# Cached keys of the second decode unit requested one unit earlier, forgetting-attention weights turned back into their row tiles

## The chip, the cores and the metric

The kernel runs on one core of a Trainium2 chip. A core has five engines that run side by side, each with its own queue of instructions, worked off in order: TensorE (PE: matmuls, and the loads of their weights, PEld), VectorE (DVE), ScalarE (ACT), GpSimd (POOL) and SyncE (SP), which here issues all DMA transfers. Engines wait for one another by semaphores. The metric is the device time of one execution, in microseconds (us); smaller is better.

## The reference

One step of a hybrid trunk of one layer, on 1024 new prompt rows and on 8 streams of 16 sample rows each, all in float32. Three token mixers run on one normalised input: a stick-breaking attention, a state-space scan (SSD) and a forgetting attention (fox). What matters here are the two attentions of the sample rows over 1024 cached rows per stream:

```python
def sb_attend(q, k, v, q_pos, k_pos):
    z = jnp.einsum('bqhd,bkhd->bhqk', q, k).astype(jnp.float32) * (HEAD_DIM ** -0.5)
    valid = k_pos[None, :] < q_pos[:, None]
    log_keep = jnp.where(valid, jax.nn.log_sigmoid(-z), 0.0)
    after = lax.cumsum(log_keep, axis=3, reverse=True) - log_keep
    w = jnp.where(valid, jnp.exp(jax.nn.log_sigmoid(z) + after), 0.0)
    return jnp.einsum('bhqk,bkhd->bqhd', w, v.astype(jnp.float32)).astype(q.dtype)

def fox_attend(q, k, v, fq, fk, q_pos, k_pos):
    s = jnp.einsum('bqhd,bkhd->bhqk', q, k).astype(jnp.float32) * (HEAD_DIM ** -0.5)
    s = s + (jnp.transpose(fq, (0, 2, 1))[..., :, None] - jnp.transpose(fk, (0, 2, 1))[..., None, :])
    valid = k_pos[None, :] <= q_pos[:, None]
    p = jax.nn.softmax(jnp.where(valid, s, -jnp.inf), axis=-1)
    return jnp.einsum('bhqk,bkhd->bqhd', p, v.astype(jnp.float32)).astype(q.dtype)
...
    logf = jax.nn.log_sigmoid((fg + p['fox_b_f']).astype(jnp.float32))
...
        sb_k = jnp.concatenate([past['sb_k'].astype(sk.dtype), sk], axis=1)
        sb_o = sb_attend(sq, sb_k, sb_v, qpos, kpos)
        fcum = jnp.cumsum(jnp.concatenate([past['fox_logf'].astype(jnp.float32), logf], axis=1), axis=1)
        fox_o = fox_attend(fq, fox_k, fox_v, fcum[:, past_len:], fcum, qpos, kpos)
```

Behind the mixers come an output projection, a cross-attention and a feed-forward part, which the change doesn't touch.

## The kernel before

In the mixed stage (which ends at about 705 us) attention units are interleaved with a filler. `mixed` makes a list of units for each attention, m = 0 stick-breaking and m = 1 fox: 16 prompt units (two blocks of 128 rows of one head each) and four decode units, whose places `AT0` and `AT1` give. A decode unit takes two streams and has two parts. `rows` computes its scores against two halves of 512 cached keys (`emit_past`) and the new ones (`emit_new`, L942 and L943), by L905 into a PSUM tile `pss`, and turns them into weights in a row tile `w` of 128 x 1152, out of a pool of seven (`ws`). `av`, a unit or two later, transposes these weights on PE (L965) into PSUM, ACT copies them out (L966), and L974 multiplies them with the cached values (`vr`, L983).

For m = 0 the cached keys are read in an arrangement of 128-byte pieces, four requests of 128 KB to a tile `kf` (L871), and DVE turns them in place (L910). A half needs two such tiles, `wh` and `wl` of one ring of three slots each, which also holds the high and low parts of the projection weights (`w_unit`: load to `wr`, L327; cast on ACT, L295; subtraction on POOL, L133) and the cached values. `fetch` asks for a unit's first half ahead of time: `mixed` hangs it on the unit in front of the decode unit. The second half is asked for in `emit_past`.

The filler `fill_s` gives the input projections in turn (fox queries and keys, `proj_v` with values and forget gates, z, the conv inputs), then the SSD scan `ssd_gen`. Behind `proj_v`, whose consumer adds the gates to `lf` (L505), `fox_sums` turns them into cumulated log gates: a logarithm in short steps on DVE (L418 to L426, with seven L424), L673, and matmuls L697 and L698 on PE; L699 copies and L705 transposes them. The matmuls of the projections are L341 to L343, three for each product of high and low parts.

Large tiles `act` (128 x 3072, six of them) hold the normalised input in its parts, the loads of the SSD blocks (L1078 to L1082), and, for each fox unit, a tile `hold` with the spread queries `qt`, the transposed weights `wt` and `wn`. For m = 0 those lie in smaller tiles (`st`, `sg2`). The tile `sc` of `ssd_gen` is a further `act` tile.

The order of each engine's queue is set by a scheduler from the program's order, priorities and modelled costs, which also gives the slots of a pool to the tiles; so a small edit can move many instructions. A load waits until the slot of its tile is free. No more than eight DMAs are on the way: each one waits for the one eight before it.

Of the kernel before, what the change touches and what calls it, by code (L numbers as in the profile page):

```python
# [8 lines left out]
F32 = mybir.dt.float32  # L9
# [8 lines left out]
P = 128  # L18
# [5 lines left out]
PAST = 1024  # L24
T = SEQ + DEC_B * DEC_S
# [38 lines left out]
def tile_hybrid_step(ctx: ExitStack, tc: tile.TileContext, a: dict):  # L64
# [22 lines left out]
    def act_t(dt=F32R, home=None):  # L87
        return (home or actp).tile([P, 3072], dt, tag="act", name="act")
# [4 lines left out]
    def st_t(dt=F32R):  # L93
        return stp.tile([P, 1024], dt, tag="st", name="st")
# [47 lines left out]
    rows = xc_t()  # L142
# [63 lines left out]
    fnew = mcst.tile([P, P], F32, name="fnew")  # L206
# [417 lines left out]
    def sg2_t(dt=F32):  # L624
        return ptp.tile([P, 256], dt, tag="so", name="so", bufs=4)
# [42 lines left out]
    fqs = mcst.tile([P, 4], F32, name="fqs")  # L668
# [189 lines left out]

    def decode_units(m):
        ck = (a["cache_sb_k"], a["cache_fox_k"])[m][0].rearrange("b k h d -> b k (h d)")
        cv = (a["cache_sb_v"], a["cache_fox_v"])[m][0].rearrange("b k h d -> b k (h d)")
# [24 lines left out]
        def rows(p):  # L888
            if not new:
                load_new()  # L890
            qsm = new[0]

            hold = act_t(F32) if m else None
            qt = (hold if m else st_t(F32))[:, 0:P]
            POOL.memset(qt, 0.0)
            q0 = qsm[:, 0:2, 0, 32 * p:32 * p + 32].rearrange("p n (b t) -> p n b t", b=2)
            qp = qt.rearrange("p (b n e t) -> p n e b t", b=2, n=2, e=2)
            for par in range(2):
                r = slice(par * 64, par * 64 + 64)
                for nb in range(2):  # L900
                    POOL.tensor_copy(qp[r, nb, par], q0[r, nb])

            def quads(ps, moving):

                together([lambda g=g: PE.matmul(ps[32 * g:32 * g + 32, :], qt[:, 32 * g:32 * g + 32],  # L905
                                                moving(g // 2, g % 2), start=True, stop=True) for g in (3, 0, 1, 2)])

            def turn_k(hf, b2):
                kf = fetched.pop((p, b2)) if (p, b2) in fetched and not hf else fetch_k(p, hf, b2)
                DVE.transpose(kf, kf)  # L910
                return kf.rearrange("c (t n i) -> c n t i", t=16, n=2)

            def load_k(hf, b2):
                rvs = []
                for q in range(2):
                    rvs.append(raw_t()[:, :512].rearrange("p (k c) -> p k c", c=256))
                    k0 = hf * 512 + q * 256

                    SP.dma_start(out=rvs[q], in_=ck[2 * p + b2, k0:k0 + 256, :].rearrange("(p k) c -> p k c", k=2))
                kf = ring.tile([P, 1088], F32, tag=("wh", "wl")[b2], name="kf")  # L920
                for q in range(2):
                    tp = pT()
                    for nb in range(2):
                        for k in range(2):
                            PE.transpose(tp[:, (2 * nb + k) * P:(2 * nb + k + 1) * P], rvs[q][:, k, nb * P:(nb + 1) * P],
                                         ident)
                    ACT.copy(kf[:, :1024].rearrange("c (n q p k) -> c n q p k", n=2, q=2, k=2)[:, :, q],
                             tp.rearrange("c (n k p) -> c n p k", n=2, k=2))
                return kf

            def emit_past(hf):
                def emit(ps):
                    if m == 0:
                        kf = [turn_k(hf, b2) for b2 in range(2)]
                        quads(ps.rearrange("p (t i) -> p t i", t=16), lambda b2, nb: kf[b2][:, nb])
                        return "turned"
                    kf = [load_k(hf, b2) for b2 in range(2)]
                    quads(ps, lambda b2, nb: kf[b2][:, nb * 512:(nb + 1) * 512])
                return emit

            def emit_new(ps):
                PE.matmul(ps, identr, dmask[:, 96 - 32 * p:224 - 32 * p], start=True, stop=False)  # L942
                together([lambda g=g: PE.matmul(ps[32 * g:32 * g + 32, :], qt[:, 32 * g:32 * g + 32], qsm[:, 2 + g % 2, 0, :],  # L943
                                                start=False, stop=True) for g in range(4)])

            pieces = [(0, 512, emit_past(0)), (512, 512, emit_past(1)), (1024, P, emit_new)]
            if m == 0:
                return sb_rows(T, pieces), hold
            fkb = xc_t()
            SP.dma_start(out=fkb[:, :PAST],  # L950
                         in_=fs4[8 * p:8 * p + 8].rearrange("r i k -> (r i) k").unsqueeze(1).to_broadcast([32, 4, PAST]))
            return fox_rows(T, pieces, [(0, PAST, fkb[:, :PAST]), (PAST, P, fnew)], fqs[:, p:p + 1], frs[:, p:p + 1]), hold

        def av(p, w, hold):
            vsm = new[1]

            wt = hold[:, P:P + 1024] if m else st_t(F32)
            wn = hold[:, P + 1024:2 * P + 1024] if m else sg2_t()[:, :P]
            for k0 in (0, 4, 8):
                nk = min(4, 9 - k0)  # L960
                tp = pT()
                for k in range(nk):
                    wk = w[:, 8 * P:9 * P] if k0 == 8 else \
                        w[:, k0 * P:(k0 + 4) * P].rearrange("q (p k) -> q p k", k=4)[:, :, k]
                    PE.transpose(tp[:, k * P:(k + 1) * P], wk, ident)  # L965
                ACT.copy(wn if k0 == 8 else wt[:, k0 * P:(k0 + 4) * P], tp[:, :nk * P])  # L966

            po = pO()

            def quads(w, moving, start, stop):  # L970
                def one(g):
                    v = moving(g // 2, g % 2)
                    out = po[32 * g:32 * g + 32, :P]
                    return PE.matmul(out if len(v.shape) == 2 else out.rearrange("p (h d) -> p h d", h=2),  # L974
                                     w[:, 32 * g:32 * g + 32], v, start=start, stop=stop)
                return [lambda g=g: one(g) for g in (3, 0, 1, 2)]

            work = quads(wn, lambda b2, nb: vsm[:, 2 * nb:2 * nb + 2, 0, :], True, False)
            for hf in range(2):
                raws = []  # L980
                for b2 in range(2):
                    raw = ring.tile([P, 1088], F32, tag=("wh", "wl")[b2], name="vr")
                    SP.dma_start(out=raw[:, :1024].rearrange("p (k c) -> p k c", c=256),  # L983
                                 in_=cv[2 * p + b2, hf * 512:(hf + 1) * 512, :]
                                 .rearrange("(p k) c -> p k c", k=4))
                    raws.append(raw)
                for k in range(4):
                    work += quads(wt[:, (4 * hf + k) * P:(4 * hf + k + 1) * P],
                                  lambda b2, nb, raws=raws, k=k: raws[b2][:, k * 256 + nb * P:k * 256 + (nb + 1) * P],
                                  False, hf == 1 and k == 3)  # L990
            together(work)
            ob = sg2_t()[:, :P]
            DVE.scalar_tensor_tensor(ob.rearrange("p (h d) -> p h d", h=2), po[:, :P].rearrange("p (h d) -> p h d", h=2),
                                     frs[:, p:p + 1] if m else 1.0, maskh.unsqueeze(2).to_broadcast([P, 2, 64]),
                                     ALU.mult, ALU.mult)
            of = pT()
            PE.matmul(of[:, :64], ob, fold2.rearrange("p n t -> p (n t)"), start=True, stop=True)
            on = sg2_t()[:, :64]
            DVE.tensor_copy(on, of[:, :64])
            SP.dma_start(out=mix_sc[2 * m:2 * m + 2, :, SEQ + 32 * p:SEQ + 32 * p + 32].rearrange("n p t -> p n t"),  # L1000
                         in_=on.rearrange("p (n t) -> p n t", n=2))

        return [([lambda p=p: rows(p)], lambda w, p=p: av(p, *w[0])) for p in range(4)], fetch


    final = []

    def ssd_gen():
        sc = act_t(F32)
        hT, gB = sc[:, 0:512], sc[:, 512:1024]  # L1010
        triu, btri, ones, bones = (sc[:, 1024 + 128 * i:1152 + 128 * i] for i in range(4))
        bmask = sc[:, 1536:1544]
# [301 lines left out]
    def mixed(m, at, fc, nxt):  # L1314
# [10 lines left out]
        units, fetch = decode_units(m)  # L1325
        for i, u in reversed(list(enumerate(units))):
            if m == 0:
                rows, av = out[at[i] - 1]
                out[at[i] - 1] = ([lambda f=rows[0], i=i: (fetch(i), f())[1]] + rows[1:], av)
            out.insert(at[i], u)  # L1330
        return out, heads[0][1]

# [837 lines left out]
```

## Time and profile before

| | |
|---|---|
| time before, three runs | 1861.90, 1858.74, 1856.07 us; median 1858.74 |
| the profiled execution | 1859.39 us, its span 1857.7 us |
| busy share of the span | PE 96%, PEld 86%, DVE 49%, ACT 42%, POOL 33% |
| DMA | 289.54 MB, 156 GB/s over the span |

The profile is of one execution. Its rows name an instruction by its line, its engine, its operation and its tiles (out<-in, without the buffers' numbers). In square brackets stands how long the engine was idle ahead of it, and what ended that. A releaser is inferred: of several semaphores it is the one that came last by the profile, and it can be the wrong one where the engine named was just passing. `SPq` is the queue of SP, in which the issues of DMAs stand. The granted clock of PE is 1.00 at full speed and about 0.5 when throttled.

### The profile page before, as it was taken

Reading aid. Unit: us, or ns where it says so; the run is one execution under the profiler, and the core shown is the slowest. Engines: PE = TensorE matmul, PEld = TensorE weight load, DVE = VectorE, ACT = ScalarE, POOL = GpSimd, SP = SyncE. Lnnn points to the kernel's source line nnn. Section 1 sums busy time; section 2 is a strip of 40 time slices with the busy share of each in tenths; the row PEclk is TensorE's granted clock in tenths of the full one; section 3 lists DMA queues with packets and bytes.
Section 4 is the critical chain, followed back from the end, with each engine's and each line's share of the span. In section 5 each row is a group of like instructions: output and inputs, shape, how many; then the busy total and the mean of one; then the engine's idle time right before and its main releaser. Section 6 shows DMA issues by size and latency. Waiting matters only on the chain.

```text
span 1857.7 us, 31848 instructions
## 1 busy us (share of the span) xinstructions
PE 1791.4 (96%) x11880; PEld 1602.9 (86%) x11880; DVE 915.9 (49%) x1808; ACT 786.5 (42%) x1665; POOL 622.0 (33%) x921
## 2 busy tenths in 40 slices
PE   7999978999998989999999989999999999999998
PEld 5899867888966767899988889999999999888886
DVE  3412434576656863455553695333333334455554
ACT  6532524445455862333342564333333333344443
POOL 7623523446115673121021107444444542000000
PEclk9999998999999999999999989999999999999999
DMA  9467765566678883257873234322222233657572
GB/s 333 160 187 185 197 140 133 149 123 194 182 236 257 284 290 103 110 138 166 191 235 105 80 93 111 90 72 72 72 72 72 72 77 88 218 187 250 177 247 86
DMA packets 367499, 289.54 MB, mean 156 GB/s; under 512 B 179052, under 2 KB 323412, under 8 KB 367344
## 3 DMA queue, kind: packets, MB, share of 16 engines
q1 hardware_dynamic: 367344, 287.50, 53.3%
q8 instruction: 94, 1.54, 0.3%
q14 instruction: 61, 0.50, 0.1%
HBM read 221.58 MB, written 66.38 MB: 155 GB/s over the span
## 4 chain that ended last, share of the span: by engine, by line
PE 79%; DVE 6%; DMA 6%; POOL 3%; ACT 2%; issue 2%; SPq 1%; DVEq 0%; POOLq 0%; ACTq 0%
PE psd L1963 11%; PE psd L341 10%; PE psd L342 9%; PE psd L343 9%; PE pst L1963 8%; PE pss L1963 4%; PE pss L341 3%; PE pss L343 3%; PE pss L342 3%; PE pso L1963 2%; PE pst L342 2%; PE pst L341 2%; PE pst L343 2%; DMA act<-acsc 1%; POOL wl L133 1%
## 5 line engine op out<-in xcount | busy, mean ns | idle before, releaser
L341 PE MATMUL psd<-act,wh 128*128 128x384 f32 x528 | 182.2, 345 | 0.0
L343 PE MATMUL psd<-act,wl 128*128 128x384 f32 x528 | 179.7, 341 | 0.0
L342 PE MATMUL psd<-act,wh 128*128 128x384 f32 x528 | 179.2, 340 | 0.0
L133 POOL TENSOR_TENSOR wl<-wr,wh 128x256 fp32r<-128x256 f32 (+2 forms) x152 | 111.6, 768 | 165.1 <-ACT wh L295 135.4
L1963 PE MATMUL pst<-bT,tr 128*128 128x256 f32 (+1 forms) x1068 | 154.6, 292 | 0.0
L1963 PEld LDWEIGHTS pst<-bT,tr 128*128 128x128 f32 x1068 | 144.6, 188 | 0.1
L343 PE MATMUL psd<-wh,act 128*128 128x512 f32 (+3 forms) x424 | 135.2, 320 | 0.0
L341 PE MATMUL psd<-wh,act 128*128 128x256 f32 (+3 forms) x414 | 132.6, 324 | 1.5 <-ACT act L1442 1.3
L342 PE MATMUL psd<-wl,act 128*128 128x256 f32 (+3 forms) x414 | 132.8, 322 | 1.2 <-POOL wl L133 1.1
L1963 PE MATMUL psd<-bT,tr 128*128 128x320 f32 (+1 forms) x912 | 132.7, 295 | 0.7 <-POOL tr L133 0.7
L1963 PEld LDWEIGHTS psd<-bT,tr 128*128 128x128 f32 x912 | 124.8, 188 | 0.9 <-POOL tr L133 0.9
L133 POOL TENSOR_TENSOR ws<-ws 128x256 f32<-128x256 f32 (+2 forms) x100 | 76.2, 788 | 133.0 <-DVE ws L538 114.5
L133 POOL TENSOR_TENSOR tr<-u,tr 128x256 fp32r<-128x256 f32 x110 | 82.9, 781 | 101.1 <-ACT tr L1799 83.3
L256 POOL TENSOR_SCALAR sm<-sm 128x1 f32<-128x1 f32 (+2 forms) x27 | 9.1, 337 | 295.4 <-ACT y L2074 207.2
L1938 DVE TENSOR_TENSOR tr<-tr,pst 128x256 f32<-128x256 f32 (+1 forms) x86 | 38.6, 449 | 138.9 <-ACT tr L1935 105.8
L341 PEld LDWEIGHTS psd<-act,wh 128*128 128x128 f32 x528 | 99.5, 188 | 4.6 <-issue 3.8
L343 PEld LDWEIGHTS psd<-act,wl 128*128 128x128 f32 x528 | 99.2, 188 | 2.2 <-issue 1.9
L342 PEld LDWEIGHTS psd<-act,wh 128*128 128x128 f32 x528 | 99.4, 188 | 1.7 <-issue 1.3
L133 POOL TENSOR_TENSOR tr<-raw,tr 128x256 fp32r<-128x256 f32 x94 | 69.2, 763 | 83.6 <-ACT tr L1799 75.4
L1799 ACT CAST tr<-u 128x512 fp32r<-128x512 f32 x130 | 76.6, 620 | 28.5 <-PE pst L1963 5.9
L341 PEld LDWEIGHTS psd<-wh,act 128*128 128x128 f32 x414 | 78.9, 191 | 9.5 <-issue 1.9
L342 PEld LDWEIGHTS psd<-wl,act 128*128 128x128 f32 x414 | 78.6, 190 | 9.2 <-POOL wl L133 3.0
(646 smaller groups left out, 4621.0 us busy)
## 6 DMA issues: line engine op xcount, KB each, us to landing
u<-w_down SPq DMA_DIRECT2D x40, 512.0 KB
raw<-w_down SPq DMA_DIRECT2D x26, 512.0 KB
st<-qksc SPq DMA_DIRECT2D x48, 256.0 KB
wr<-w_in SPq DMA_DIRECT2D x44, 256.0 KB
tr<-hidsc SPq DMA_DIRECT2D x55, 192.0 KB
hidsc<-tr SPq DMA_DIRECT2D x34, 288.0 KB
qksc<-sg SPq DMA_DIRECT2D x48, 192.0 KB
kf<-cache_sb_k SPq DMA_DIRECT2D x64, 128.0 KB
```

What stands on the lines that cost most here:

```text
L133: POOL.tensor_tensor(out=out[:, a0:a1], in0=in0[:, a0:a1], in1=in1[:, a0:a1], op=op)
L256: POOL.tensor_scalar(v, ss, inv, EPS, ALU.mult, ALU.add)
L341: PE.matmul(out, ah, bh, start=start, stop=False)
L342: PE.matmul(out, ah, bl, start=False, stop=False)
L343: PE.matmul(out, al, bh, start=False, stop=stop)
L1799: ACT.copy(hi, src)
L1938: DVE.tensor_tensor(out=at(out, g), in0=at(x, g), in1=ps[g][:, :GW[g]], op=op)
L1963: PE.matmul(dst[g][:, :GW[g]], x[:, ka], y[:, k, :], start=start and k == 0 and m == 0, stop=stop and k == 3 and m == 2, skip_group_check= ...
```

## The change

Three edits. The fetch of the first half of keys for stick-breaking decode unit 1 (and this unit only) hangs on the unit two in front of it, not one. `av` copies the transposed weights back into the columns of the unit's own row tile `w`, from which they were transposed. And there is no `hold` tile: the fox queries `qt` lie in 128 columns, one of two places in turn, of a single `act` tile which `ssd_gen` uses as `sc`.

```diff
+    kept = []
+
+    def keep_t():
+        if not kept:
+            kept.append(act_t(F32))
+        return kept[0]
...
-            hold = act_t(F32) if m else None
-            qt = (hold if m else st_t(F32))[:, 0:P]
+            qt = keep_t()[:, 2456 + P * (p % 2):2456 + P * (p % 2) + P] if m else st_t(F32)[:, 0:P]
...
-        def av(p, w, hold):
+        def av(p, w):
             vsm = new[1]
-
-            wt = hold[:, P:P + 1024] if m else st_t(F32)
-            wn = hold[:, P + 1024:2 * P + 1024] if m else sg2_t()[:, :P]
+            wt, wn = w[:, 0:8 * P], w[:, 8 * P:9 * P]
...
     def ssd_gen():
-        sc = act_t(F32)
+        sc = keep_t()
...
             if m == 0:
-                rows, av = out[at[i] - 1]
-                out[at[i] - 1] = ([lambda f=rows[0], i=i: (fetch(i), f())[1]] + rows[1:], av)
+                k = at[i] - (2 if i == 1 else 1)
+                rows, av = out[k]
+                out[k] = ([lambda f=rows[0], i=i: (fetch(i), f())[1]] + rows[1:], av)
```

The number of instructions stays the same on every engine. By the trace of before, the orders differ between about 205 and 350 us and between 470 and 705 us. Lines of the changed kernel are 4 to 7 higher: L871 is L878, L910 is L916, L1000 is L1004, L1078 is L1082, L919 is L925.

On SP, behind the loads of z's first weights (220 us in the trace of before), where the keys of unit 1 were not yet in sight:

```order
L327 DMA wr<-w_in 128x2x256
L327 DMA wr<-w_in 128x2x8
L520 DMA st<-qksc 64x1024
L521 DMA st<-qksc 64x1024
L327 DMA wr<-w_in 128x2x256
L327 DMA wr<-w_in 128x2x8
L1000 DMA mixsc<-so 128x2x32
```

and in the changed kernel:

```order
L327 DMA wr<-w_in 128x2x256
L327 DMA wr<-w_in 128x2x8
L878 DMA kf<-cache_sb_k 32x32x32 x4
L1004 DMA mixsc<-so 128x2x32
L878 DMA kf<-cache_sb_k 32x32x32 x4
L327 DMA wr<-w_in 128x2x256
L327 DMA wr<-w_in 128x2x8
```

The eight requests of the first half now stand here, four on either side of the store of unit 0's result. Before, they stood behind the stores of proj_v, at 256 us.

On DVE, the logarithm of the forget gates, first as before (260 to 269 us):

```order
L422 TENSOR_SCALAR sg<-sg 128x36
L910 STREAM_TRANSPOSE kf<-kf 128x1024
L424 SCALAR_TENSOR_TENSOR sg<-sg 128x36 x7
L425 SCALAR_TENSOR_TENSOR sg<-sg 128x36
L910 STREAM_TRANSPOSE kf<-kf 128x1024
L426 TENSOR_SCALAR sg<-sg 128x36
L711 SCALAR_TENSOR_TENSOR sg<-sg 128x64 x4
L673 SCALAR_TENSOR_TENSOR lf<-lf,sg 128x36
```

and in the changed kernel, from the fourth of the seven L424 on:

```order
L424 SCALAR_TENSOR_TENSOR sg<-sg 128x36
L916 STREAM_TRANSPOSE kf<-kf 128x1024
L716 TENSOR_TENSOR so<-so,smask 128x32
L424 SCALAR_TENSOR_TENSOR sg<-sg 128x36 x3
L425 SCALAR_TENSOR_TENSOR sg<-sg 128x36
L426 TENSOR_SCALAR sg<-sg 128x36
L673 SCALAR_TENSOR_TENSOR lf<-lf,sg 128x36
L693 COPY so<-lf 128x4
L916 STREAM_TRANSPOSE kf<-kf 128x1024
```

The two transposes that stood in this chain were of the first half of keys; the ones that stand there now are of the second half. The two of the first half moved up, to either side of an L538 and ahead of two L505.

On SP, the load of an SSD block that left at 544 us before:

```order
L1058 DMA acsc<-so 72x128
L622 DMA mixsc<-so 64x256
L816 DMA zsc<-sg 128x256
L1080 DMA act<-acsc 128x1024
L1082 DMA act<-zsc 128x512
L520 DMA st<-qksc 64x1024
L521 DMA st<-qksc 64x1024
L622 DMA mixsc<-so 64x256
L1078 DMA act<-xbcsc 128x8x128
```

and in the changed kernel (where L1058 is L1062, L1080 is L1084 and L1082 is L1086):

```order
L816 DMA zsc<-sg 128x256
L520 DMA st<-qksc 64x1024
L521 DMA st<-qksc 64x1024
L1062 DMA acsc<-so 72x128
L1082 DMA act<-xbcsc 128x8x128
L622 DMA mixsc<-so 64x256
L1086 DMA act<-zsc 128x512 x2
L1084 DMA act<-acsc 128x1024 x2
```

It now stands right behind L1062 and has no wait for L974.

More of the change, by code (lines that the diff above doesn't have):

```diff
@@ L947, in rows @@
             if m == 0:
-                return sb_rows(T, pieces), hold
+                return sb_rows(T, pieces)
             fkb = xc_t()
@@ L951, in rows @@
                          in_=fs4[8 * p:8 * p + 8].rearrange("r i k -> (r i) k").unsqueeze(1).to_broadcast([32, 4, PAST]))
-            return fox_rows(T, pieces, [(0, PAST, fkb[:, :PAST]), (PAST, P, fnew)], fqs[:, p:p + 1], frs[:, p:p + 1]), hold
-        def av(p, w, hold):
+            return fox_rows(T, pieces, [(0, PAST, fkb[:, :PAST]), (PAST, P, fnew)], fqs[:, p:p + 1], frs[:, p:p + 1])
+        def av(p, w):
             vsm = new[1]
-            wt = hold[:, P:P + 1024] if m else st_t(F32)
-            wn = hold[:, P + 1024:2 * P + 1024] if m else sg2_t()[:, :P]
+            wt, wn = w[:, 0:8 * P], w[:, 8 * P:9 * P]
             for k0 in (0, 4, 8):
@@ L1001, in av @@
                          in_=on.rearrange("p (n t) -> p n t", n=2))
-        return [([lambda p=p: rows(p)], lambda w, p=p: av(p, *w[0])) for p in range(4)], fetch
+        return [([lambda p=p: rows(p)], lambda w, p=p: av(p, w[0])) for p in range(4)], fetch
     final = []
     def ssd_gen():
-        sc = act_t(F32)
+        sc = keep_t()
         hT, gB = sc[:, 0:512], sc[:, 512:1024]
```

## The prediction

> **What bounds the kernel now.** First the page: how busy each engine is, and the chain that ended last.
>
> ```profile
> PE 1791.4 (96%) x11880; PEld 1602.9 (86%) x11880; DVE 915.9 (49%) x1808; ACT 786.5 (42%) x1665; POOL 622.0 (33%) x921
> PE 79%; DVE 6%; DMA 6%; POOL 3%; ACT 2%; issue 2%; SPq 1%; DVEq 0%; POOLq 0%; ACTq 0%
> ```
>
> TensorE (PE) is busy for 1791.4 of 1857.7 us, so all its holes together are 66 us. The change leaves the matmuls as they are: it can win only holes and stretches at a low clock. Windows of 50 us say where these lie among the ones that the change reaches (columns: window, length, PE busy and its instructions, PEld, DVE, ACT, POOL, granted clock, DMA share, GB/s).
>
> ```profile
> 250.00:300.00 50.00, 34.87 (x268) 26.83 (x267) 21.88 (x53) 18.20 (x40) 16.74 (x27) 0.89 0.66 144
> 500.00:550.00 50.00, 46.45 (x389) 35.66 (x388) 24.03 (x87) 24.33 (x57) 7.83 (x17) 0.97 0.81 248
> 550.00:600.00 50.00, 44.08 (x384) 32.56 (x382) 33.45 (x99) 32.27 (x74) 25.13 (x44) 1.00 0.82 253
> 600.00:650.00 50.00, 48.88 (x416) 38.42 (x417) 41.27 (x119) 38.47 (x89) 33.42 (x53) 1.00 0.86 283
> 650.00:700.00 50.00, 43.89 (x340) 32.95 (x338) 34.67 (x81) 31.82 (x61) 33.06 (x49) 1.00 0.87 291
> ```
>
> 250 to 300 us alone lacks 15.1 us, at a clock of 0.89. The waits of PE between 200 and 320 us name most of it (us in total, times, longest):
>
> ```profile
> PE pss L905 <- DVE sg L426: 5.9, 1, 5.9
> PE pss L905 <- DMA wr<-w_in: 3.9, 1, 3.9
> PE pst L965 <- POOL ws L133: 1.9, 2, 1.8
> ```
>
> L905 is the score product of cached unit 1, and its real releaser is its keys. The next rows show it, on PE, then SyncE (SP), then VectorE (DVE), each in order of time (start, duration):
>
> ```profile
> 267.28 2.03 PE L905 MATMUL pss<-kf,st 128*32 128x512 f32 x8 [5.90 <-DVE sg L426]
> 269.24 0.64 PE L697 MATMUL psd<-lf,sg 128*128 128x32 f32 x2
> 274.18 0.28 PE L341 MATMUL psd<-wh,act 128*128 128x264 f32 x1
> 279.00 2.03 PE L905 MATMUL pss<-kf,st 128*32 128x512 f32 x8 [3.85 <-DMA wr<-w_in]
> 282.47 0.37 PE L341 MATMUL psd<-wh,act 128*128 128x264 f32 x1
> ...
> 256.18 2.92 SPq L871 DMA_DIRECT2D kf<-cache_sb_k  x4
> 259.89 3.01 SPq L871 DMA_DIRECT2D kf<-cache_sb_k  x4
> 264.87 3.09 SPq L871 DMA_DIRECT2D kf<-cache_sb_k  x4
> 269.48 5.08 SPq L871 DMA_DIRECT2D kf<-cache_sb_k  x4
> ...
> 262.39 1.25 DVE L910 STREAM_TRANSPOSE kf<-kf 128x1024 f32<-128x1024 f32 x1 [1.66 <-DMA kf<-cache_sb_k]
> 265.98 1.25 DVE L910 STREAM_TRANSPOSE kf<-kf 128x1024 f32<-128x1024 f32 x1 [0.66 <-DMA kf<-cache_sb_k]
> 267.15 0.14 DVE L426 TENSOR_SCALAR sg<-sg 128x36 f32<-128x36 f32 x1
> 267.95 0.17 DVE L673 SCALAR_TENSOR_TENSOR lf<-lf,sg 128x36 f32<-128x36 f32 x1
> 277.70 1.25 DVE L910 STREAM_TRANSPOSE kf<-kf 128x1024 f32<-128x1024 f32 x1 [4.87 <-DMA kf<-cache_sb_k]
> ```
>
> Four groups of four requests stand one behind the other, and each transpose starts 3.1 to 3.3 us after the end of its group (259.10 to 262.39, 262.90 to 265.98, 274.56 to 277.70). The second ends at 267.23 and L905 starts at 267.28; the fourth starts at 277.70 and L905 follows. L426, named in the row, is only what DVE did next. SP starts at 256.18 because weights of proj_v hold the ring slots of the keys: the first row below is that wait of SP. The others are windows after such holes, with a clock of about a half (columns as above).
>
> ```profile
> SPq L871 <- PE psd L343: 7.3, 1, 7.3
> ...
> 265.40:272.20 6.80, 4.92 (x22) 3.26 (x23) 4.57 (x18) 2.86 (x4) 1.60 (x3) 0.51 0.76 116
> 279.00:282.50 3.50, 3.50 (x22) 1.14 (x22) 0.65 (x3) 1.40 (x2) 0.00 (x0) 0.53 0.23 36
> 541.90:545.30 3.40, 3.40 (x47) 2.37 (x39) 1.94 (x7) 1.03 (x2) 0.00 (x0) 0.52 0.00 1
> ```
>
> **The first half of unit 1's keys.** In the changed order their eight requests stand ahead of z's second weights and wait only for the value products of unit 0 (L974).
>
> ```profile
> 221.82 1.93 PE L974 MATMUL pso<-vr,st 128*32 128x128 f32 x64
> 232.50 0.42 DVE L505 TENSOR_TENSOR lf<-psd,hb 128x4 f32<-128x4 f32 x2
> 234.66 0.37 PE L341 MATMUL psd<-wh,act 128*128 128x260 f32 x1
> 269.34 0.63 ACT L295 CAST wh<-wr 128x528 fp32r<-128x528 f32 x1 [8.67 <-PE pss L905]
> ```
>
> L974 ends at 223.75. The first group goes out by 226.7, the second, behind a store (L1000), by some 230.8, and 3.2 us later its transpose runs, 234.0 to 235.3. Both L505 stand behind it on DVE and move from 232.5 to 235.7. The matmul at 234.66 waits for them, since its accumulator must be read first: **+1.2 us**, between 0 (keys 1.5 us sooner) and 3 (2 us later, as the group that took 5.08 instead of 3). L905's eight matmuls now run right behind, at full clock, in 1.1 us. So proj_v ends 2.3 us later than before.
>
> The casts of z's first weights (L295) get the slots that these keys had and now wait for L905, and SP's next weight loads and some stores of v rows wait behind those casts. Not before 269.69 does z begin, over 30 us later: that hides it; bare, z would wait for two casts of 0.63 us and their subtractions on GpSimd, 5 us at most.
>
> **What takes the place of the 5.90 us wait.** L697 stands next on PE. It needs the sums of the forget gates, which end with L673: at 268.1 before, only 0.9 us after the keys. So a second wait lay under the first. In the new order one transpose of the second half's keys stands inside this chain on DVE, behind four of seven L424 steps. These requests still wait for proj_v's weights: they start at about 258.4, four stores and a load stand between them, and the fourth goes out by 263.6. The transpose runs 3.2 us later, 266.8 to 268.0, then come seven steps of 0.14 to 0.2 us: L673 ends at 269.6 and **L697 starts at 269.8, 0.6 us later than now**. PE arrives at 263.7 and waits 6 us. The hole keeps its size and changes its name. Between ends: 268.3 (no transpose in the way, as before) and 271.8 (the group takes 5.08 us).
>
> z's matmuls behind it run as before, about half of them at the low clock: 274.3 where 274.46 was.
>
> **The second half's keys.** The last group now goes out by 266.5 instead of 274.56 and is turned by 271. L905 needs it at 274.3, so the 3.85 us wait goes: it starts 4.7 us before 279.00. With no idle time ahead of it, the slow clock of 279.0 to 282.5 goes too: 3.5 us of work take 1.9, and 1.1 us of small matmuls that came sooner before now follow (L698, L705 and two of z). At the same point of the work PE stands **5.2 us** ahead. L965's wait of 1.78 is a chain from these scores through ScalarE (ACT), DVE and GpSimd (POOL); it moves with them, and I take 0.3 us of it. Sum of this stretch: **-5.5 us**, from -8.5 (nothing at L505, L697 at 268.3) to -1.7 (L505 at 3, L697 at 271.8).
>
> The Trainium skill, "TensorE: Matmul & The Clock Gate" (What's actually happening), says that an idle window of about 3.4 us halves the clock and that it takes as long a busy one to bring it back. The windows at 265.4 and 279.0 agree, after holes of 5.90 and 3.85 us. By this rule the hole that stays before L697 keeps its slow stretch, as my sum has it; if it kept the clock, the sum would be 2 us better.
>
> **No large tile for the fox weights.** The copies (L966) are as many and as large as before and lie on ACT, busy for 42%; bare, one of 512 columns costs 0.59 us (first row). What goes is the wait of SP for a free large tile. Its row is of the whole span, the others are waits of PE between 470 and 705 us:
>
> ```profile
> L966 ACT COPY st<-pst x8: 587/596/635, 216.6 to 445.4; 128x512 f32<-128x512 f32 x8
> ...
> SPq L1078 <- PE pso L974: 12.2, 2, 9.7
> ...
> PE psd L1095 <- DMA act<-xbcsc: 2.2, 2, 2.0
> PE psd L1135 <- ACT sg L1210: 2.1, 1, 2.1
> PE pso L974 <- ACT act L966: 1.5, 1, 1.5
> ```
>
> One load of an SSD block, and all behind it on SP, can go up to 9.7 us sooner. But PE waits only 2.2 us for such loads, and in both orders the one behind the 2.0 stands after a store of state (L1187), not after the tile. The four windows from 500 to 700 lack 16.7 us of PE in all, in small waits, and the slow clock at 541.9 costs 1.6. All engines' orders are shuffled here, so each wait may go or be replaced. Bounds: -8 (half of the waits gone) and +6 (three more of 2 us, the size of those above). I take **-3**: the 1.5 for L966 with the slow stretch behind it, the row nearest to the edit. For the columns shared in one kept tile I take 0: the two copies of qt alternate, and each is read before the unit after next writes it.
>
> Sum: 1859.39 of the profiled execution - 5.5 - 3.0 = 1850.9. That execution lies 0.65 us above the median of the runs, so I say 1850.3.
>
> **Rivals.** Full cure: the sums end before PE comes, and both holes and both slow stretches go. For it: L673's own chain is short steps. Against it: DVE runs in order, and a transpose that waits for late keys stands in the middle. It gives 5.9 + 3.85 + 4 of lost clock (half of 4.92 + 3.5) - 1.2 = 12.6, with 3 of the fox stage 1843.
>
> No change that can be told: the second half lands as late as the group of 5.08, L505 costs 3, and the fox stage gives nothing; or the moved requests find no slot before proj_v ends, so that the change does not do what it says. For it: DMA shares of 0.81 to 0.87 in the fox stage leave loads little to gain. Against the second: the order names L974 as their wait. It gives 0 to -3: 1857.
>
> Slower: the weights go back into the score tile, so one of seven `ws` tiles is held until the value products have read it, not only until it is transposed.
>
> ```profile
> 536.95 0.33 PE L965 MATMUL pst<-identr,ws 128*128 128x128 f32 x1
> ...
> 541.10 3.04 PE L974 MATMUL pso<-vr,act 128*32 128x128 f32 x64
> ```
>
> For fox unit 0 that is 537.3 to 544.1, 6.8 us, and 27 us for four. A unit whose rows wait for the tile leaves PE only the SSD blocks. For it: the new order has waits of ACT for L974 (at L536 and L558). Against: seven tiles rotate, and by the trace's times L974 is mostly long done. With nothing exposed it costs 0; from 14 of the 27 us on the result is slower by over 5.6. It gives about 1866.
>
> **How the numbers follow.** 0.3% is 5.6 us, about what a measurement can tell. Forecast (1845 to 1853): 0.50. Full cure: 0.08. No change: 0.28. Slower: 0.14. So faster 0.58, same 0.28, slower 0.14. The range takes in the forecast with its bounds and the third case, and leaves half of the first rival and most of the last out: 1844 to 1861.
>
> **What would show it.** Right: L905's first eight matmuls lie near 237 us; L697, not L905, carries a wait of about 6 us up to 270; the second L905 follows z without a wait, and its eight matmuls take 1.1 us; L1078 waits no more for L974. Wrong: L697 waits under 2 us or over 8; L505 holds PE for more than 3 us near 235; or the fox stage changes by more than 6 us either way.

## The result and the profile after

The changed kernel takes 1872.46 us, the median of five runs (1871.53 to 1875.02), beside 1858.74 for five of the kernel before measured with it (1854.47 to 1866.06): a ratio of 1.0077, with 95% between 1.006 and 1.0095. It is 13.7 us slower, where 8.4 faster was forecast, and above the range. The profiled execution has 1871.94 us and a span of 1870.1. The line of busy time on its page has the same counts of instructions as before, and hardly more work:

```profile
PE 1795.2 (96%) x11880; PEld 1607.4 (86%) x11880; DVE 925.2 (49%) x1808; ACT 787.2 (42%) x1665; POOL 623.0 (33%) x921
```

PE is busy 3.8 us longer and idle for 8.6 us more (74.9 of the span against 66.3).

To see where the time goes, the matmuls of each trace were added up in order, each weighted by the median duration of its kind in the trace of before (where matmuls overlap, the time that one adds). The table, a calculation on the traces, says how far a kernel's PE stands behind that of before at the same sum of work (+ is late, us; the head is the time in the trace of before). Its values are good to about 1 us.

| | 200 | 260 | 280 | 380 | 460 | 540 | 580 | 620 | 680 | 720 | 1800 |
|---|---|---|---|---|---|---|---|---|---|---|---|
| changed kernel | +1.0 | +6.3 | +1.8 | +0.3 | +3.5 | +3.6 | +7.2 | +9.6 | +15.9 | +13.8 | +12.9 |
| fetch alone (e1) | +0.4 | +3.7 | -2.1 | -2.1 | -2.5 | -1.0 | -4.1 | -3.8 | -4.4 | -5.2 | -4.5 |
| last unit alone (e12) | +2.1 | +2.5 | +5.0 | +2.1 | +3.5 | +4.9 | +9.2 | +9.8 | +24.5 | +22.8 | +21.5 |
| changed, but for the last unit (e14) | +2.0 | +5.9 | +0.1 | +0.5 | +2.3 | +0.7 | +5.1 | +5.0 | +10.7 | +8.2 | +7.0 |

(The last three rows are of experiments below.) Two things went wrong in the changed kernel. The stretch from 200 to 380 us was to win 5.5 and won 0.7. And the mixed stage behind 440 us, which was to win 3, lost 12: by the same sum the changed kernel stands 1.6 us behind at 440 us.

**The first stretch** is seen in the changed kernel on PE, on DVE and on SP, each in order of time (start, duration, in brackets the idle time ahead and what ended it; L911 and L916 are L905 and L910 of before):

```profile
238.57 0.39 PE L341 MATMUL psd<-wh,act 128*128 128x260 f32 x1 [0.84 <-DVE lf L505]
240.32 1.07 PE L911 MATMUL pss<-kf,st 128*32 128x512 f32 x8
...
273.60 0.60 PE L697 MATMUL psd<-lf,sg 128*128 128x32 f32 x2 [6.62 <-DVE lf L673]
...
279.13 1.19 PE L911 MATMUL pss<-kf,st 128*32 128x512 f32 x8
...
263.83 0.16 DVE L505 TENSOR_TENSOR lf<-psd,hb 128x4 f32<-128x4 f32 x1 [2.69 <-ACT so L501]
...
269.65 0.65 DVE L711 TENSOR_TENSOR_SCAN sg<-sg 128x64 f32<-128x64 f32 x3 [1.53 <-DMA sg<-cache_fox_logf]
...
270.89 1.25 DVE L916 STREAM_TRANSPOSE kf<-kf 128x1024 f32<-128x1024 f32 x1
...
273.26 0.20 DVE L673 SCALAR_TENSOR_TENSOR lf<-lf,sg 128x36 f32<-128x36 f32 x1
...
261.94 2.04 SPq L878 DMA_DIRECT2D kf<-cache_sb_k  x3
264.08 0.74 SPq L408 DMA_DIRECT2D s_fox_v<-so  x1
```

Every step that was forecast is there: the first scores inside `proj_v`, a short wait for L505, then 6.62 us before L697 (6 forecast), and second scores that start without a wait and take 1.19. But all of it is later than forecast: L697 by 3.8 us and the second scores by 4.8 (274.3 was said), so that these now stand where they stood before, at 279.

**The mixed stage**, in the window from 440 to 720 us of before, of the changed kernel, and of two experiments (e12, then e14; columns as in the prediction, so after the length PE busy, and the granted clock as the third number from the end):

```profile
440.00:720.00 280.00, 263.30 (x2072) 211.82 (x2071) 179.09 (x484) 158.09 (x351) 123.99 (x204) 0.99 0.74 234
```
```profile
440.00:720.00 280.00, 256.83 (x2020) 206.39 (x2019) 182.82 (x482) 155.74 (x345) 120.29 (x197) 0.96 0.73 232
```
```profile
440.00:720.00 280.00, 258.44 (x1985) 208.15 (x1983) 171.87 (x469) 152.84 (x340) 119.07 (x197) 0.93 0.73 227
```
```profile
440.00:720.00 280.00, 265.32 (x2048) 211.35 (x2047) 186.46 (x485) 156.07 (x348) 121.73 (x197) 0.96 0.73 232
```

The changed kernel is idle 23.2 us here against 16.7: 6.5 more. Its clock is 0.96 against 0.99; busy time by what the clock lacks is 10.3 us against 2.6, so 7.6 more are lost by a slower PE that counts as busy (an estimate from the two columns: the clock is rounded to 0.01, which is 2.6 us). Together 14, of which the table shows 12. In e12 it is 4.9 and 15.5, in e14 -2.0 and 8.0. The two can change places, so I read their sum: e13, an experiment whose orders are those of before in this stretch, has 4.8 us less idle time and 5.4 more by the clock.

```profile
440.00:720.00 280.00, 268.06 (x2073) 216.60 (x2072) 182.06 (x489) 158.21 (x351) 121.94 (x198) 0.97 0.74 233
```

The idle part has a name in the waits of PE in this window (us in total, times, longest), first before, then after:

```profile
PE pst L925 <- DMA wr<-cache_fox_k: 1.4, 1, 1.4
```
```profile
PE pst L931 <- DMA wr<-cache_fox_k: 9.7, 4, 3.5
```

These are transposes of cached fox keys (L925 before, L931 after) that wait for their loads. They are not what parts slow kernels from others, though: e3 has 8.7 us of these waits and e18 9.0, and neither can be told from before, while e2 has 3.4 and is slower by 0.89%. The lost clock is seen in a window of 10 us, before and after, and in the rows of the transposes of an SSD block in it (L1170, after L1174):

```profile
550.00:560.00 10.00, 8.97 (x58) 4.93 (x56) 7.49 (x28) 7.51 (x16) 0.84 (x2) 1.00 0.98 263
...
551.08 1.11 PE L1170 MATMUL pst<-identr,act 128*128 128x128 f32 x8
```
```profile
550.00:560.00 10.00, 9.22 (x37) 5.36 (x37) 4.37 (x16) 3.48 (x6) 0.00 (x0) 0.53 0.95 238
...
552.44 0.76 PE L1184 MATMUL psd<-act 32*128 32x256 f32 x1 [0.78 <-DVE sm L562]
...
553.60 1.97 PE L1174 MATMUL pst<-identr,act 128*128 128x128 f32 x8
555.49 1.22 PE L1184 MATMUL psd<-act 32*128 32x256 f32 x2
556.64 1.97 PE L1174 MATMUL pst<-identr,act 128*128 128x128 f32 x8
```

PE is busy for 9.0 and 9.2 us, but does 58 matmuls in the one and 37 in the other; eight transposes take 1.97 us instead of 1.11. The view of waits shows nothing of that; the column of the clock and the durations do. But this slow window is not peculiar to the slow kernels either. From 550 to 560 us e14 has a clock of 0.50 and e13, with the orders of before here, 0.58, and neither can be told from before. The rows of one execution show where its time went, not yet which edit sent it there; that is for the experiments.

### The profile page after: what moved, and what is told of

Read it like the earlier page. It is cut to its first block, busy times and chain, and to the rows that moved or that the text cites. A ratio compares the mean times of both kernels' runs of the same rounds, so it can differ in the third digit from the quotient of the medians.

```text
span 1870.1 us, 31817 instructions
## 1 busy us (share of the span) xinstructions
PE 1795.2 (96%) x11880; PEld 1607.4 (86%) x11880; DVE 925.2 (49%) x1808; ACT 787.2 (42%) x1665; POOL 623.0 (33%) x921
## 4 chain that ended last, share of the span: by engine, by line
PE 81%; DVE 7%; DMA 5%; POOL 3%; issue 2%; ACT 2%; SPq 1%; DVEq 0%; POOLq 0%; ACTq 0%
PE psd L1968 11%; PE psd L341 10%; PE psd L342 9%; PE psd L343 9%; PE pst L1968 8%; PE pss L1968 3%; PE pss L341 3%; PE pss L343 3%; PE pss L342 3%; PE pso L1968 2%; PE pst L341 2%; PE pst L342 2%; PE pst L343 2%; PE pso L609 1%; PE pst L594 1%
## 5 line engine op out<-in xcount | busy, mean ns | idle before, releaser
L341 PE MATMUL psd<-act,wh 128*128 128x384 f32 x528 | 182.0, 345 | 1.3 <-ACT xc L764 1.3
L341 PE MATMUL psd<-wh,act 128*128 128x256 f32 (+3 forms) x414 | 134.0, 328 | 2.1 <-DVE dts L818 0.9
L341 PEld LDWEIGHTS psd<-act,wh 128*128 128x128 f32 x528 | 99.5, 188 | 6.1 <-issue 3.8
L341 PEld LDWEIGHTS psd<-wh,act 128*128 128x128 f32 x414 | 79.8, 193 | 9.9 <-issue 1.5
```

Of the source, the lines that this page charges most:

```text
L341: PE.matmul(out, ah, bh, start=start, stop=False)
```

## The experiments

Ratios are to runs of the kernel before on the same chip (its median there 1858 to 1861 us), with 95% intervals; they are estimated over all runs and need not be the quotient of the two medians. Four questions were put, in this order.

**Which part of the change costs time?** The fetch alone (e1, the last hunk of the diff in the kernel before); everything but the fetch (e2); and only the `hold` tile gone, with the weights of both attentions in the small tiles (e3):

```diff
-            wt = hold[:, P:P + 1024] if m else st_t(F32)
-            wn = hold[:, P + 1024:2 * P + 1024] if m else sg2_t()[:, :P]
+            wt, wn = st_t(F32), sg2_t()[:, :P]
```

> The kernel before with one edit alone: the first-half keys of decode unit 1 are asked for one unit earlier; hold tiles and weight copies stay as before, and the orders differ from before only up to about 350 us. Theory T1 (the 13.7 us are lost in the fox stage by the tile edits; the moved fetch is worth about nothing): within 3 us of before, 1857 to 1862, and no change of order or waits behind 400 us. Rival T2 (the moved fetch shifts the work and the fox stage pays for it): 1866 to 1873. My blind prediction had this stretch at -5.5 us, 1853.

> The changed kernel with the fetch back at the unit right ahead, so the tile edits alone (weights back into the row tile, no hold tile). T1: 1870 to 1874, nearly all of the loss, with the late fox-key loads (waits of about 10 us for cache_fox_k in all) as in the changed kernel. T2: 1857 to 1862.

> Of the tile edits one part: no hold tile (queries in columns of the kept tile), but the transposed weights go to small tiles (st and sg2) for both attentions, as stick-breaking had it before. Theory T1a (the loss comes since a score tile is held until the value products): within 4 us of before, 1855 to 1862. Theory T1b (the loss comes since the freed large tiles let SSD loads go sooner and shuffle the fox stage): 1867 to 1874.

| | us | ratio |
|---|---|---|
| e1 | 1862.96 | 1.0014 (0.9988 to 1.0041) |
| e2 | 1875.55 | 1.0089 (1.0058 to 1.0119) |
| e3 | 1864.38 | 1.0028 (0.9998 to 1.0057) |

So the loss is in the edit of the tiles. What dropping `hold` costs can't be told from nothing, though its interval reaches 0.57%, and e3's time lies between the two ranges expected. The fetch is worth nothing that ten runs could tell. The profiled execution of e1 (1854.48 us), one of the lowest of ten from 1852.85 to 1870.68, shows what the table's second row says: 2.1 us ahead behind the second scores, not 5.5.

**Whose weights?** e4 puts the weights of both attentions into `w` and leaves fox a large tile of its own for the queries; e5 does the fox weights alone, e6 the stick-breaking weights alone, both with `hold`. e7 holds `w` as long as e5 does, for a third of the copies only:

```diff
 e5
+            wt = w[:, 0:8 * P] if m else st_t(F32)
+            wn = w[:, 8 * P:9 * P] if m else sg2_t()[:, :P]
 e6
+            wt = hold[:, P:P + 1024] if m else w[:, 0:8 * P]
+            wn = hold[:, P + 1024:2 * P + 1024] if m else w[:, 8 * P:9 * P]
 e7
-                ACT.copy(wn if k0 == 8 else wt[:, k0 * P:(k0 + 4) * P], tp[:, :nk * P])
+                ACT.copy(wn if k0 == 8 else (w if m and k0 == 4 else wt)[:, k0 * P:(k0 + 4) * P], tp[:, :nk * P])
...
-                    work += quads(wt[:, (4 * hf + k) * P:(4 * hf + k + 1) * P],
+                    work += quads((w if m and hf else wt)[:, (4 * hf + k) * P:(4 * hf + k + 1) * P],
```

> The other part: the transposed weights go back into the score tile, but a large tile is still taken for the queries of each fox unit, and the SSD scan has its own. T1a: 1867 to 1874. T1b: 1855 to 1862. If both parts lose about half, neither tile alone is the cause.

> The kernel before with one edit: fox units copy the transposed weights back into their score tile; their hold tile stays, with the queries alone in it, and stick-breaking units are as before. The edit of the score tile was worth +17 us for both attentions together. If the fox units carry the loss (theory T1a, held score tiles in the stage where PE has little else to do): 1868 to 1875. If the stick-breaking units do: 1857 to 1863.

> The counterpart: only stick-breaking units copy back into their score tile. In the runs with both, the work of PE fell behind by 1.6 us near 390 and 1.7 near 450 us, where these units stand. T1a: 1859 to 1864, some 3 us. If these units carry the loss: 1868 to 1875.

> As the kernel before, with the hold tile, but of a fox unit's three groups of transposed weights only the second (512 of 1152 columns, the one that the products read last) goes back into the score tile; the others stay in the hold tile. So the score tile is held to the end of the products as in e5, while most copies go where they went before. If holding the tile is the cause: as e5, within 4 us. If it is the copies into the tile (their size or their place): a third to a half of the loss of e5.

| | us | ratio |
|---|---|---|
| e4 | 1876.80 | 1.0096 (1.0065 to 1.0127) |
| e5 | 1871.41 | 1.0041 (1.002 to 1.0061) |
| e6 | 1877.21 | 1.0081 (1.0054 to 1.0109) |
| e7 | 1865.58 | 1.0021 (0.9999 to 1.0044) |

e6 has as much as the whole loss. Fox, of which the change is named, has about half of it when it is edited alone (e5, inside the range expected if fox carried the loss), so the two parts do not add up. e7 lies between before and e5 and can't be told from before, with an interval that overlaps that of e5, so it doesn't settle whether the held tile or the copies cost the fox units their share. The traces speak against the tile: a row tile that is held too long would let a write into it wait for L974, and between 200 and 720 us e5 has no such wait of ACT, DVE or POOL. The rival of the prediction (fox row tiles held too long) thus looked at the smaller part.

**Which of the four stick-breaking units?** e13 does units 0 to 2 alone, e12 unit 3 alone, e14 is the changed kernel with unit 3 as before, and e15 takes from unit 3 only the small tile:

```diff
 e13 (e12 has p == 3 for p < 3)
+            wt = hold[:, P:P + 1024] if m else w[:, 0:8 * P] if p < 3 else st_t(F32)
+            wn = hold[:, P + 1024:2 * P + 1024] if m else w[:, 8 * P:9 * P] if p < 3 else sg2_t()[:, :P]
 e14
+            wt = st_t(F32) if m == 0 and p == 3 else w[:, 0:8 * P]
+            wn = sg2_t()[:, :P] if m == 0 and p == 3 else w[:, 8 * P:9 * P]
 e15
+            wn = hold[:, P + 1024:2 * P + 1024] if m else w[:, 8 * P:9 * P] if p == 3 else sg2_t()[:, :P]
```

> The counterpart: the first three stick-breaking units copy back into their score tiles, the last one as before. The orders of all engines stay those of before, only the tiles' names differ, though three score tiles are held longer. T3: as before, 1857 to 1862. T1a: three quarters of the loss, 1869 to 1873.

> The kernel before; only the last of the four stick-breaking decode units copies its transposed weights back into its score tile. In the orders, this is the one unit whose edit moves other work: its value products (L974) go up some 90 matmuls, and all engines' orders change from there to the end of the fox stage. Theory T3 (the loss is the new order that begins with this unit's earlier products, not a held tile): 1870 to 1878, as the run with all stick-breaking units. Rival T1a (held score tiles, each unit some): a quarter of that loss, 1862 to 1865.

> The changed kernel with the last stick-breaking unit's weights in small tiles again; the other units, the fox units and the moved fetch as changed. T3: most of the loss goes, 1857 to 1865 (the fox units alone cost some 5 us, the fetch nothing that could be told). T1a: at least three quarters of the loss stay, 1869 to 1873.

> The kernel before; of the last stick-breaking unit only the third, small group of transposed weights (128 of 1152 columns) goes back into the score tile, so only the small tile (sg2) is not taken. Its value products then move up in the order as in the run with all its weights. If it is this tile that held them back in the schedule of before (T3, sharper): 1870 to 1878. If the large small-tile (st) matters: within 4 us of before.

| | us | ratio |
|---|---|---|
| e13 | 1867.03 | 1.0017 (0.9992 to 1.0042) |
| e12 | 1881.07 | 1.0112 (1.0077 to 1.0147) |
| e14 | 1862.81 | 1.0013 (0.9993 to 1.0033) |
| e15 | 1873.12 | 1.0067 (1.0044 to 1.0089) |

Unit 3 decides. Its edit alone costs more than the whole change (1.12% beside 0.77, with intervals that overlap), the changed kernel without it can't be told from the kernel before, and the 128 columns of its small tile alone cost 0.67%. In e13 three units hold their row tile until the products have read it, and it can't be told from the kernel before either. Its median lies between the two ranges expected, but three quarters of e6's loss would be 0.61%, and its interval ends at 0.42. The traces agree that holding costs little: the only write into a row tile that waits for L974 between 200 and 720 us is L536 on ACT, once, for 1.8 us in the changed kernel and 1.2 in e13, and never in e12. The orders of e13 differ from those of before at few places (131 of 11034 on PE, all ahead of the 2150th), and at none in the mixed stage behind 440 us; e12's differ at 860 of PE's, all from the 2526th on. PE's first rows that differ in e12, beside the kernel before (+ are those of e12):

```
 L576 MATMUL pss<-st 128x512
 L577 MATMUL pss<-st 128x512
+L974 MATMUL pso<-pt,ws 32x128 x4
+L974 MATMUL pso<-vr,ws 32x128 x16
 L576 MATMUL pss<-st 128x512
 L577 MATMUL pss<-st 128x512
```

With no small tile to wait for, the value products of this unit are put between scores of a prompt unit. In e15, which spares only the tile of 128 columns, PE's first row that differs is the same L974 at the same place. In the traces they move by 7 us, before, then e12 (the changed kernel has 445.34 as well):

```profile
452.44 0.42 PE L974 MATMUL pso<-pt,so 128*32 128x128 f32 x8
```
```profile
445.33 0.42 PE L974 MATMUL pso<-pt,ws 128*32 128x128 f32 x8
```

From there the queues of all engines differ at many places until the mixed stage ends.

**Was the fetch hidden under the next wait?** L697 stands next on PE, and its sums come from `proj_v`; z, which stands behind L697, needs neither keys nor sums. e8 is e1 with z's first product ahead of the sums, in `fill_s`; e9 has this swap alone, e17 has it in the changed kernel, e18 in e14:

```diff
-        next(sums)
-        yield
-        next(zs)
-        yield
+        next(zs)
+        yield
+        next(sums)
+        yield
```

> The moved fetch alone (as e1), and in the filler each step of z's projection is put ahead of a step of the forget-gate sums, so that PE has z's first block while the sums run. In e1 PE waited 6.3 us for the sums (L697). If that wait is all that is left of the hole: it falls by 3 us or more, with its slow clock after it, and the stretch of 250 to 300 us gains 3 to 6 us on e1, 1850 to 1858. If the wait only moves again (keys, or z's weights): as e1.

> The kernel before with z's steps ahead of the steps of the forget-gate sums, and the fetch where it was. Theory T2' (the moved fetch gave too little because the wait for the sums, L697, took the hole over; both are needed): without the moved fetch PE still waits for unit 1's first keys up to about 267 us, so within 4 us of before, 1855 to 1863. If the order of z and sums alone is worth the 10 us of e8: 1848 to 1853, and the moved fetch is worth nothing in any company.

> The changed kernel, complete, with z's steps ahead of the sums. If the two halves of the change act apart (the fetch up to 300 us, the last stick-breaking unit's weights behind 440 us): the gain of about 7 us that e8 has over e1 comes on top of the changed kernel's 1872, so 1863 to 1868. If the fox stage loses whatever is won ahead of it: 1870 to 1874.

> The changed kernel with z's steps ahead of the sums and the last stick-breaking unit's weights in small tiles. If both repairs add: 1850 to 1857, at least as good as e8. If the fox units' edits cost their 5 us here: 1855 to 1860, and e8 stays the best.

| | us | ratio |
|---|---|---|
| e8 | 1852.65 | 0.9945 (0.9922 to 0.9967) |
| e9 | 1862.21 | 0.9986 (0.9967 to 1.0005) |
| e17 | 1869.37 | 1.003 (1.0008 to 1.0053) |
| e18 | 1861.41 | 0.9988 (0.9965 to 1.001) |

e8 is faster than the kernel before by an interval that leaves 1 out, and so than the changed kernel; neither of its halves alone is. Its waits of PE in this stretch have no L697; one long wait is left, for the second half of keys (the second L910 of DVE behind them ends at 274.86):

```profile
274.91 2.14 PE L905 MATMUL pss<-kf,st 128*32 128x512 f32 x8 [8.44 <-DMA wr<-w_in]
277.97 0.64 PE L697 MATMUL psd<-lf,sg 128*128 128x32 f32 x2
```

It is a long one, but it covers the chain of the sums as well, and only one hole is left of two. The pair e18 and e8 says that the other edits of the change, without unit 3, cost about 0.4% beside it, with intervals that overlap a little. e17 is slower than before by 0.30%, so the swap wins about 0.5% in the changed kernel too (1.0077 without it), and unit 3's edit costs about 0.4% there beside e18; its 1869.37 us lie between the two ranges expected.

## Why the prediction was wrong

**The step that failed is "No large tile for the fox weights: I take -3", with its bounds of -8 and +6.** The term had the wrong sign: behind 440 us the change cost 12. Three things in it were wrong.

- It looked at fox, where the change speaks of itself, and at the place where an SSD load no longer waits for L974. That wait did go, and no run shows that it won anything (e3, without `hold`, is not faster than before). The wait of L974 for L966, from which the -3 was taken, went as well, and others came. The loss came from stick-breaking unit 3, whose small tiles the same line of `av` takes away; the prediction has no word on it. The order it rested on was said to differ from 470 us on; behind 440 us the first row of PE that differs is the L974 of this unit, at 445 us.
- Its upper bound was "three more of 2 us, the size of those above". In the changed kernel the late loads of fox keys alone have four waits and 9.7 us.
- It counted holes. By the estimate above 7.6 us of 14, and in e12 15.5 of 20, are lost by a low clock, in stretches such as that at 550 us. Rows of waits give no bound for that.

How the earlier products lead to that is not settled. Shown is that this one edit changes the order from 445 us on and that the loss lies behind; no run isolates which of the moved rows makes it, and neither the late fox keys nor the slow window at 550 us tells the slow kernels from the others. The loss of e12 is larger than that of the change, and e14 is 7 us late in its profiled execution though its median is not: what such a shuffle costs seems to depend on all the rest of the order, which no run tries by itself.

**The slower rival** (row tiles held too long) had the right sign and a chance of 0.14, but not the mechanism that the runs show. It spoke of fox units, which cost 0.41% (0.2 to 0.61) in e5 when they are changed alone, without a wait for a held tile; and three units that hold their tiles cost nothing that e13 could tell. That it came closest in time is luck.

**The fetch: right in its steps, wrong in its size.** The forecast was -5.5; e1's profiled execution has -2.1 to -2.5, the changed kernel -0.7, and the runs of e1 show no difference. In the changed kernel the term that was mis-sized is how late `proj_v` ends: 2.3 us were said. The last L505, which ends it, ran at 258.06 before and runs at 263.83 in the changed kernel, 5.8 later, and the sums follow it: L673 went from 267.95 to 273.26. I had taken that chain as held up by keys; with the first half gone from it, it waits for `proj_v`, and in its middle DVE waits 1.53 us for cached log gates (L711). Most of the excess of 3.5 us is there when PE comes to L505: the L341 behind it starts at 238.57, where 235.9 was said. The moved fetch does not explain that, since in e1 this L341 starts as forecast:

```profile
235.91 0.39 PE L341 MATMUL psd<-wh,act 128*128 128x260 f32 x1 [0.95 <-DVE lf L505]
```

In the changed kernel 1.0 us stood at 200 us already, and the rest came by a wait of PE for POOL, and the slow clock behind it (e1 has a clock of 1.00 in this window). So the large group of L974 of unit 0 (L978 there), which frees the keys' slots, starts at 224.59 instead of 221.82, and the keys, their transposes and L505 follow:

```profile
220.62 0.39 PE L342 MATMUL psd<-wl,act 128*128 128x260 f32 x1 [1.24 <-POOL wl L133]
...
220.00:230.00 10.00, 9.38 (x116) 8.61 (x117) 2.96 (x5) 3.75 (x8) 7.72 (x14) 0.83 0.40 84
```

The second half of keys was requested from 261.94 on instead of 258.4, behind stores of `proj_v` on SP, so nothing of the shift was won back.

In e1 this term is nearly right: the last L505 runs at 261.17, 3.1 later than before, and L697 at 270.80, 1.0 later than forecast. What else is missing there lies behind the second scores, where the prediction counts only on 0.3 us of one wait. Between 278 and 335 us PE waits 4.1 us for L536 on ACT, beside 1.8 before, and 1.7 us in three waits that before hasn't (L341, L705, L997). Against that, the waits of L965 (1.9, with the 0.3) and of L974 (0.5) are gone. That makes some 2 us, and with the 1 us of L697 it is the 3 us between -5.5 and -2.5.

**The rule on the clock.** The prediction let the hole before L697 keep its slow stretch, after the Trainium skill, "TensorE: Matmul & The Clock Gate" (What's actually happening). The trace agrees: the matmuls of 264 columns behind it take 0.42 us, those of 260 ahead of it 0.28:

```profile
263.06 0.28 PE L343 MATMUL psd<-wh,act 128*128 128x260 f32 x1
...
274.60 0.42 PE L343 MATMUL psd<-wh,act 128*128 128x264 f32 x1
```

**That one wait would take the place of another** was right, and e8 shows its price: fetch and swap together win 0.55%, and the fetch of this about 0.4% by e9, where the swap is alone (with intervals that touch).

## What to carry to other kernels

Where a scheduler sets the order, a tile that is no longer taken is a change of order, not of space: look for the first row that differs on each engine, ask whose tile held it there, and try that unit alone, since here the edit of one unit of eight cost more by itself than the whole change. A wait that goes is worth what the next wait on the same engine leaves of it; if that one hangs on the same producer, move independent work between the two. And price a stretch with few matmuls twice, by its holes and by the clock in the windows behind them; and before you name a wait as the cause, look for it in kernels that are not slower.

## What the runs showed of the hardware

A stretch that the profile counts as busy need not bring the clock back. In e2 the low clock that the changed kernel has at 550 us lasts longer; windows of 4 us show it:

```profile
556.00:560.00 4.00, 4.00 (x16) 3.02 (x15) 1.35 (x5) 1.51 (x3) 0.00 (x0) 0.50 1.06 274
560.00:564.00 4.00, 4.00 (x18) 1.64 (x16) 0.70 (x2) 1.63 (x4) 0.00 (x0) 0.50 0.37 106
564.00:568.00 4.00, 4.00 (x14) 1.57 (x13) 3.13 (x10) 1.01 (x2) 0.89 (x2) 0.50 0.48 145
568.00:572.00 4.00, 4.00 (x17) 2.69 (x16) 2.05 (x9) 1.63 (x4) 0.52 (x1) 0.50 0.40 133
...
576.00:580.00 4.00, 4.00 (x33) 3.33 (x32) 2.28 (x5) 1.35 (x4) 2.38 (x5) 1.00 0.84 249
```

PE has no idle time in them, yet the clock stays at 0.50 for the 16 us of the first four. The page of the Trainium skill named above gives about 3.4 us of sustained activity as what restores it; the measurement decides: here 16 us that the profile counts as busy (with ends of matmuls that are modelled) did not. Between 556 and 572 us PE ran mostly small matmuls (L1184 with 32 rows, L1177 on 32 columns, some transposes); whether that is the reason no run tries by itself. They do not lower the clock by themselves: the kernel before runs the same lines (L1180 and L1173 there) between 550 and 560 us at 1.00, as the row of that window above shows.

The time of one kernel goes with its mean granted clock. Beside e1, the kernel before ran 22 times, from 1853.10 us at a clock of 0.991 to 1873.29 at 0.984. The 0.007 between them, over some 1791 us of busy PE, are 12.5 of the 20 us. Under such a spread ten runs of the fetch alone could not tell 2 us from none.
